# Attention output divided from a DRAM copy of the turned factors: twelve of sixteen divisions

## The chip, the cores and the metric

The kernel runs on one core of a Trainium2 chip. A core has five engines that run side by side, each with its own instruction order: TensorE (PE, with its weight loads shown as PEld), VectorE (DVE), ScalarE (ACT), GpSimd (POOL) and SyncE (SP), which here only issues transfers. They work on one on-chip memory (SBUF, 128 partitions) and on PSUM, the accumulators into which PE writes; DRAM is reached by DMA. The metric is the device time of one execution in microseconds (us). The kernel before takes 1926.52 us, the median of three runs (1925.0, 1926.52 and 1926.74).

## The reference

The model is a two-layer decoder trunk over 1024 tokens of width 1024: a short convolution with a SwiGLU mixer, then sliding-window attention with a SwiGLU mixer, all in float32. The change lies in the attention. There are 16 query heads of width 64, 4 key and value heads, a window of 128 tokens, a linear distance bias, and one learned logit per head (the sink) that takes part in the softmax and is then dropped:

```python
scores = jnp.einsum('bnqkgd,bnskd->bnkgqs', qb, kw).astype(jnp.float32) * scale
scores = scores + alibi[None, None]
scores = jnp.where(mask[None, :, None, None], scores, -jnp.inf)
logits = jnp.concatenate([scores, sink_col], axis=-1)
p = jax.nn.softmax(logits, axis=-1)[..., :-1]
out = jnp.einsum('bnkgqs,bnskd->bnqkgd', p.astype(vw.dtype), vw)
return out.reshape(bsz, s, N_Q_HEADS * HEAD_DIM) @ w_o
```

The kernel computes the exponents without dividing, multiplies them with the values, and divides the result afterwards by the sum of the exponents and the sink. This division is what the change rewrites.

## The kernel before, in words

Float32 products are made from pairs of a rounded high part and a low part (hi, lo), three matmuls for each product of two such pairs. The large matrix products also use a scheme with seven block products in place of eight.

**Layout.** Activations lie with features on the partitions and tokens along the free axis. Two heads make one tile i (0 to 7), two tiles make a pair p (0 to 3), and 1024 tokens make 8 blocks b of 128. The attention outputs of a pair lie in `O[p, h]` for each half h of the tokens (4 blocks).

**Steps.** The attention stage runs through 64 units (i, b), one for each step n, so a pair takes 16 steps. An order written out by hand, `ORDER = "SPTMEDkPHLVOPK"`, says what a step issues, and all engines keep the order in which they are issued (a manual schedule). S are the scores of unit n (PE, L2231 and L2232), M the row maxima (DVE, L2246), E the exponents of unit n-1 with their row sums (ACT, L2266), T the transposes of unit n-2 (PE, L2274) into one of the PSUM banks P1 and P3, in turn; the other of the two is called free in that step. H and L are the hi and lo parts of what T turned (ACT, L2281; DVE, L2287). V is the product with the values of unit n-3 (PE, L2300 and L2301) and O its copy into `O[p, h]` (ACT, L2318; DVE, L2319). Each P is a piece of other work for PE: the query product of a later pair (L1997), which from step 46 on gives way to the output product (L172, L176). D runs the list of this step's divisions, and k and K run work that was planned for this half or whole step: the normalisation of queries (L1803, L1808, L1813), the splitting of weight granules into hi (DVE, L1940) and lo (POOL, L1941), and of query tiles into hi (ACT, L2164) and lo (POOL, L2169).

**One division before.** A division takes a pair p, a half h of the tokens and a quarter k, at step n = 16p + 16 + 6h + 2k. At n-4 the sink goes into the sum (POOL, ACT, POOL; L2329 to L2331, only for k = 0). At n-2 DVE takes the reciprocal of the sums (L2336, 128x16, only for k = 0), and POOL spreads the factors over 512 columns in a buffer `s1` (L1803): query on the partitions, one column for each head and feature. At n PE turns that with four 128x128 transposes (L1808) into the free bank, and DVE multiplies `O` by what stands in the bank (L2347). The normalisation of the queries uses the same transposes, with a multiply by DVE (L1813).

**Transfers.** SP issues the operand loads of the query product (L2455, 512 KB from `q_ops` each) and the granules of the weights (L1934, 256 KB each). SP issues a transfer once its waits are over, and what stands behind waits with it. ACT issues none in this stage.

Of the kernel before, what the change touches and what calls it, by code (L numbers as in the profile page):

```python
# [47 lines left out]
SUB = P // 2  # L48
# [30 lines left out]
HALF = T // 2  # L79
# [9 lines left out]
def trunk_kernel(ctx: ExitStack, tc: tile.TileContext, xT, small, w_in, w_out, w_q, w_v, w_o, w_gu, w_dn, out):  # L89
    nc = tc.nc  # L90
    sb = ctx.enter_context(tc.tile_pool(name="sb", bufs=1))
    pm = ctx.enter_context(tc.tile_pool(name="pm", bufs=1, space=bass.MemoryType.PSUM))
    dve, act, pool, pe = nc.vector, nc.scalar, nc.gpsimd, nc.tensor
    uid = [0]

    def slot(tag, shape=(P, D), dtype=F32, bufs=1):
        uid[0] += 1
        return sb.tile(list(shape), dtype, tag=tag, name=f"{tag}_{uid[0]}", bufs=bufs)
# [107 lines left out]
    ident = cst[:, C_ID : C_ID + P]  # L206
# [1453 lines left out]
    def attention_layer():  # L1660
# [48 lines left out]
        def head_newton(y, t, m):  # L1709
            dve.scalar_tensor_tensor(t, t, -0.5, m, ALU.mult, ALU.mult)  # L1710
            dve.scalar_tensor_tensor(y, t, 1.5, y, ALU.add, ALU.mult)

        it = {}
        v = []
        summed = {}
# [183 lines left out]
        sums = {}  # L1899
# [421 lines left out]
        def divide_steps(p, h, k):  # L2321

            it = {}

            def sink():

                t = least[p, h]
                tiles = sinks[:, 2 * p : 2 * p + 2]
                pool.tensor_tensor(t, t, tiles.unsqueeze(1).to_broadcast([P, 8, 2]), ALU.subtract)  # L2329
                act.activation(t, t, AF.Exp)  # L2330
                pool.tensor_tensor(sums[p, h], sums[p, h], t, ALU.add)  # L2331

            def wide():
                d = sums[p, h]
                if k == 0:
                    dve.reciprocal(d, d)  # L2336
                it["wide"] = slot("s1", (P, HALF))
                spread(pool, it["wide"], d[:, 4 * k : 4 * k + 4, :])

            def rows():  # L2340
                it["ps"] = bank(pos["free"])
                turn_blocks(it["ps"], it["wide"])

            def scale():
                c = slice(k * 2 * P, (k + 1) * 2 * P)
                o = O[p, h][:, :, c].rearrange("p e (s q) -> p s e q", q=SUB)
                dve.tensor_tensor(o, o, it["ps"].rearrange("p (s e q) -> p s e q", s=4, q=SUB), ALU.mult)  # L2347

            return wide, rows, scale, sink


        due = {}
        divisions = {}
        for p in range(NK // 2):
            for h in (0, 1):
                for k in (0, 1):
                    *steps, sink = divide_steps(p, h, k)
                    divisions[p, h, k] = wide, rows, scale = steps
                    n = 16 * p + 16 + 6 * h + 2 * k
                    if k == 0:  # L2360
                        due.setdefault(n - 4, []).append(sink)
                    due.setdefault(n - 2, []).append(wide)
                    due.setdefault(n, []).extend([rows, scale])
        for n in due:
            due[n].sort(key=lambda f: f.__name__ == "wide")

# [2 lines left out]
        pos = {"n": -LAG, "step": 0, "free": "P1", "piece": 0, "values": None}  # L2369
        agenda = {}  # L2370

        def plan(d, f):

            agenda.setdefault(pos["step"] + d, []).append(f)
# [120 lines left out]
        with tc.manual_schedule(engines={E.PE, E.Activation, E.DVE, E.Pool, E.SP}):  # L2495
# [19 lines left out]
            todo = [late[0], late[1]]  # L2515
            free = ["XS4", "XS7"]
            first_w = {}
            for m in range(NK):
                acc = Acc()
                work = product(acc, w, o_split, len(early))  # L2520
                for k in range(len(early)):
                    if m + 1 < NK and k == 0:
                        w_next = Weights()
                        w_next.load(w_o[m + 1][:, 0 : len(early), :], 0, len(early))
                    if todo and pos["n"] >= 2 * NB * (todo[0] // 2 + 1) + 8:
                        split_o(todo.pop(0), free.pop(0), 0)
                    if m == NK - 1 and k == 0:
                        for t, tag in ((NK - 2, "XS0"), (NK - 1, "XS2")):
# [22 lines left out]
        for e in (0, 1):  # L2551
            wide, rows, scale = divisions[NK // 2 - 1, 1, e]
# [117 lines left out]
```

## Time and profile before

| | before |
|---|---|
| median of three runs | 1926.52 us |
| the profiled execution, own time | 1927.2 us |
| its span | 1925.2 us |
| PE busy | 1915.5 us (99%) |
| DVE busy | 1326.6 us (69%) |
| ACT busy | 894.0 us (46%) |
| POOL busy | 306.1 us (16%) |
| attention steps with divisions of pairs 0 to 2 | 1074 to 1204 us of the span |

The prediction reads the profile of this one execution. A group of instructions is named by its line, its engine and what it writes and reads. Behind a row, [0.43 <-DVE mx L2246] says that the engine sat idle for 0.43 us before this instruction, and that the wait ended with DVE's line 2246. In a timeline a row with x4 is four instructions in a run, with the time from the first start to the last end.

### The profile page before, as it was taken

How to read it: one execution, taken by the hardware profiler on the slowest of the kernel's cores; microseconds unless marked ns; L12 is line 12 of the kernel's file. 1: busy time of each engine (PE TensorE's matmuls, PEld its weight loads, DVE VectorE, ACT ScalarE, POOL GpSimd, SP SyncE). 2: the span in 40 equal slices, each digit the busy share in tenths (PEclk: the TensorE clock that was granted, in tenths of full speed). 3: DMA queues.
4: the chain of work that ended last, by engine and by line, in shares of the span. 5: the costliest groups of instructions: out<-in, count | busy, mean ns of one | idle time of the engine just before them, and what ended most of it. 6: DMA issues, size and time to landing. Idle time of an engine off the chain costs nothing.

```text
span 1925.2 us, 25420 instructions
## 1 busy us (share of the span) xinstructions
PE 1915.5 (99%) x9045; PEld 1599.9 (83%) x9045; DVE 1326.6 (69%) x2293; ACT 894.0 (46%) x1753; POOL 306.1 (16%) x391
## 2 busy tenths in 40 slices
PE   9999999999999999999999999999999999999999
PEld 7888888888888888888887888888888888888887
DVE  8997877975665666655866887788756665665543
ACT  5543464633333334444557787655333333344441
POOL 0011231011111100000015556310111111100000
PEclk9999999999999999999998999999999999999999
DMA  8897595387898638986364661242675575477562
GB/s 317 258 249 157 128 250 156 114 269 210 230 250 231 155 135 293 323 251 207 108 253 141 207 215 56 78 153 80 218 211 139 199 190 164 133 246 273 197 229 100
DMA packets 154910, 374.13 MB, mean 194 GB/s; under 512 B 15392, under 2 KB 26784, under 8 KB 154784
## 3 DMA queue, kind: packets, MB, share of 16 engines
q1 hardware_dynamic: 119392, 263.16, 39.8%
q0 software_dynamic: 35248, 109.33, 23.2%
q8 instruction: 71, 1.16, 0.2%
q14 instruction: 55, 0.45, 0.1%
q10 hardware_dynamic: 144, 0.03, 0.0%
HBM read 300.89 MB, written 149.42 MB: 234 GB/s over the span
## 4 chain that ended last, share of the span: by engine, by line
PE 95%; DVE 2%; ACT 2%; issue 1%; POOL 0%; DMA 0%; POOLq 0%; DVEq 0%; ACTq 0%
PE acc L1004 16%; PE acc L1007 16%; PE acc L1005 16%; PE P L1004 10%; PE P L1007 10%; PE P L1005 10%; PE acc L172 2%; PE acc L1997 2%; PE P L1997 2%; PE acc L176 1%; PE P L2274 1%; PE P L1678 1%; PE acc L1137 1%; PE acc L1139 1%; PE acc L1138 1%; PE P L1808 1%
## 5 line engine op out<-in xcount | busy, mean ns | idle before, releaser
L1004 PE MATMUL acc<-XS,G 128*128 128x512 f32 x926 | 360.4, 389 | 0.0
L1007 PE MATMUL acc<-XS,G 128*128 128x512 f32 x926 | 360.3, 389 | 0.0
L1005 PE MATMUL acc<-XS,G 128*128 128x512 f32 x926 | 360.2, 389 | 0.0
L1004 PE MATMUL P<-A,G 128*128 128x512 f32 x550 | 214.1, 389 | 0.0
L1007 PE MATMUL P<-A,G 128*128 128x512 f32 x550 | 214.0, 389 | 0.0
L1005 PE MATMUL P<-A,G 128*128 128x512 f32 x550 | 214.0, 389 | 0.0
L1007 PEld LDWEIGHTS acc<-XS,G 128*128 128x128 f32 x926 | 173.8, 188 | 36.2
L1005 PEld LDWEIGHTS acc<-XS,G 128*128 128x128 f32 x926 | 173.9, 188 | 36.0
L1004 PEld LDWEIGHTS acc<-XS,G 128*128 128x128 f32 x926 | 173.9, 188 | 35.9
L1004 PE MATMUL acc<-A,G 128*128 128x512 f32 x442 | 172.1, 389 | 0.0
L1007 PE MATMUL acc<-A,G 128*128 128x512 f32 x442 | 172.0, 389 | 0.0
L1005 PE MATMUL acc<-A,G 128*128 128x512 f32 x442 | 171.9, 389 | 0.0
L938 DVE TENSOR_TENSOR G<-WL,G 128x512 fp32r<-128x512 f32 x168 | 115.1, 685 | 73.5 <-ACT G L937 73.5
L938 DVE TENSOR_TENSOR G<-WR,G 128x512 fp32r<-128x512 f32 (+1 forms) x216 | 144.3, 668 | 29.3 <-ACT G L937 29.1
L937 ACT CAST G<-WR 128x512 fp32r<-128x512 f32 (+1 forms) x216 | 130.5, 605 | 63.2 <-PE acc L1007 30.7
L937 ACT CAST G<-WH 128x512 fp32r<-128x512 f32 (+1 forms) x174 | 104.7, 601 | 85.1 <-PE acc L1007 43.9
L1339 ACT ACTIVATE G<-G 128x512 f32<-128x512 f32 x88 | 55.8, 634 | 159.0 <-DVE G L1436 153.1
L938 DVE TENSOR_TENSOR G<-WH,G 128x512 fp32r<-128x512 f32 (+1 forms) x174 | 115.5, 664 | 20.4 <-ACT G L937 20.3
L1004 PEld LDWEIGHTS P<-A,G 128*128 128x128 f32 x550 | 103.3, 188 | 21.5 <-DVE G L548 0.2
L1007 PEld LDWEIGHTS P<-A,G 128*128 128x128 f32 x550 | 103.3, 188 | 21.5
L1005 PEld LDWEIGHTS P<-A,G 128*128 128x128 f32 x550 | 103.3, 188 | 21.3
L901 POOL DMA_DIRECT2D s<-s x68 | 60.0, 892 | 361.0 <-DMA s<-s 177.9
(414 smaller groups left out, 3806.1 us busy)
## 6 DMA issues: line engine op xcount, KB each, us to landing
G<-h SPq DMA_DIRECT2D x70, 512.0 KB, 4.8
s<-in_w_dn SPq DMA_DIRECT2D x32, 704.0 KB, 8.2
h<-X POOLq DMA_DIRECT2D x44, 512.0 KB, 5.2
s<-s POOLq DMA_DIRECT2D x32, 704.0 KB, 7.1
WR<-s SPq DMA_DIRECT2D x79, 256.0 KB, 3.9
WR<-in_w_gu SPq DMA_DIRECT2D x36, 512.0 KB, 5.2
WH<-in_w_gu SPq DMA_DIRECT2D x36, 512.0 KB, 4.6
XS<-q_ops SPq DMA_DIRECT2D x36, 512.0 KB, 5.3
```

The source lines that it names most:

```text
L172: pe.matmul(ps.half(h), wh, xs[:, j, c], start=first and j == 0, stop=False)
L176: pe.matmul(ps.half(h), wl, xs[:, 0, c], start=False, stop=last)
L901: nc.gpsimd.dma_start(dst[to], dst[of], accum_op=ALU.add)
L937: lambda: act.copy(out_hi, raw),
L938: lambda: lo_eng.tensor_tensor(out_lo, raw, plain(out_hi), ALU.subtract),
L1004: pe.matmul(ps, w[:, 0, c], x[:, 0, :], start=start and e == 0, stop=False, skip_group_check=True)
L1005: pe.matmul(ps, w[:, 0, c], x[:, 1, :], start=False, stop=False, skip_group_check=True)
L1007: pe.matmul(ps, w[:, 1, c], x[:, 0, :], start=False, stop=last, skip_group_check=True)
L1137: pe.matmul(ps, hi[:, kc], xs[:, 0, c], start=k == 0, stop=False, skip_group_check=True)
L1138: pe.matmul(ps, hi[:, kc], xs[:, 1, c], start=False, stop=False, skip_group_check=True)
L1339: state["silu"] = act.activation(x, x, AF.Silu)
L1997: pe.matmul(ps, g[:, w, c], x[:, b, :], start=begin and i == 0, stop=end and i == 2, skip_group_check=True)
```

## The change

The twelve divisions of pairs 0, 1 and 2 take another way; the four of the last pair stay. At n-3 DVE takes the reciprocal into a small buffer of its own (`hr_z`, 128x16). Half a step later PE turns it with one transpose into 16 rows of 128 (L1716 of the changed file), ACT copies it from PSUM into an `s1` buffer (L1718), and ACT's queue writes it to DRAM (L1719, 8 KB). One step after the reciprocal SP reads it back with two transfers (L1725), each of which gives one row of 512 factors to 64 partitions. The second quarter is read at n-1. POOL multiplies `O` by the buffer, at n+1 for the first quarter and at n+2 for the second. The spreading copies on POOL, the groups of four transposes and the multiplies on DVE are gone for these twelve. Two late splits of the output tiles wait for two more steps.

```diff
+        def rows_to_dram(columns, room, dst):
+            ps = bank(pos["free"])
+            pe.transpose(ps[0 : 2 * NB, 0:P], columns.rearrange("p h b -> p (h b)"), ident)
+            turned = room[0 : 2 * NB, 0:P]
+            act.copy(turned, ps[0 : 2 * NB, 0:P])
+            nc.scalar.dma_start(dst, turned)
+
+        def rows_from_dram(out, src, c=slice(0, D)):
+            for h in (0, 1):
+                row = src[h * NB : (h + 1) * NB].rearrange("b c -> (b c)")[c]
+                nc.sync.dma_start(out[h * HD : (h + 1) * HD, :], row.unsqueeze(0).to_broadcast([HD, row.shape[0]]))
...
             def scale():
                 c = slice(k * 2 * P, (k + 1) * 2 * P)
                 o = O[p, h][:, :, c].rearrange("p e (s q) -> p s e q", q=SUB)
-                dve.tensor_tensor(o, o, it["ps"].rearrange("p (s e q) -> p s e q", s=4, q=SUB), ALU.mult)
-
+                eng, by = (pool, it["wide"]) if divided_by_dma(p, h) else (dve, it["ps"])
+                eng.tensor_tensor(o, o, by.rearrange("p (s e q) -> p s e q", s=4, q=SUB), ALU.mult)
+
+            def inverse():
+                inv = slot("hr_z", (P, 2, NB), bufs=2)
+                dve.reciprocal(inv.rearrange("p i s -> p s i"), sums[p, h])
+                rows_dram[p, h] = tc.dram_tile((2 * NB, P), F32, name=f"rows_d{p}_{h}")
+                plan(0.5, lambda: rows_to_dram(inv, slot("s1", (P, HALF)), rows_dram[p, h]))
+                plan(1, fetch)
+
+            def fetch():
+                it["wide"] = slot("s1", (P, HALF))
+                rows_from_dram(it["wide"], rows_dram[p, h], slice(k * HALF, (k + 1) * HALF))
+
+            if divided_by_dma(p, h):
+                return inverse, fetch, scale, sink
             return wide, rows, scale, sink
...
+        def divided_by_dma(p, h):
+            return p < NK // 2 - 1
...
-                    due.setdefault(n - 2, []).append(wide)
-                    due.setdefault(n, []).extend([rows, scale])
+                    if not divided_by_dma(p, h):
+                        due.setdefault(n - 2, []).append(wide)
+                        due.setdefault(n, []).extend([rows, scale])
+                    elif k == 0:
+                        due.setdefault(n - 3, []).append(wide)
+                        due.setdefault(n + 1, []).append(scale)
+                    else:
+                        due.setdefault(n - 1, []).append(lambda f=rows: plan(0, f))
+                        due.setdefault(n + 2, []).append(scale)
...
-                    if todo and pos["n"] >= 2 * NB * (todo[0] // 2 + 1) + 8:
+                    if todo and pos["n"] >= 2 * NB * (todo[0] // 2 + 1) + 10:
```

In the instruction orders below, each row has the line, the operation, the buffer written and the buffers read, and the shape; lines of the changed file from 1712 on stand 14 or more higher than in the file before. `cst` is the identity for a transpose, `acc` and `P0` to `P3` are PSUM banks.

The first place is PE in step 20, which turns a normalisation of the queries (the group of four into P1, fed from G6). Before:

```order
L1997 MATMUL acc_1195_8416<-XS5_1115_7592,WL_1139_7846 128x512 x2
L2274 MATMUL P3_1307_9219<-cst_1_61,s0_1188_8369 128x128 x4
L1808 MATMUL P1_1310_9232<-cst_1_61,G6_1279_9037 128x128 x4
L1997 MATMUL acc_1195_8416<-XS5_1115_7592,WL_1139_7846 128x512
L1997 MATMUL acc_1195_8416<-XS7_1118_7619,WL_1139_7846 128x512
```

After the change:

```order
L2011 MATMUL acc_1195_8416<-XS5_1115_7592,WL_1139_7846 128x512 x2
L2288 MATMUL P3_1309_9220<-cst_1_61,s0_1188_8369 128x128 x4
L1822 MATMUL P1_1311_9231<-cst_1_61,G6_1282_9045 128x128 x4
L1716 MATMUL P1_1315_9242<-cst_1_61,hr_z_1302_9191 16x128
L2011 MATMUL acc_1195_8416<-XS5_1115_7592,WL_1139_7846 128x512
L2011 MATMUL acc_1195_8416<-XS7_1118_7619,WL_1139_7846 128x512
```

The single transpose of the factors stands right behind the group of four and writes the same bank P1. The same holds in step 36 for the next pair.

The second place is ACT in step 14. Before:

```order
L2266 ACTIVATE G2_1187_8368,den_1227_8630<-G2_1187_8368,mx_1223_8596 128x192 x2
L1973 COPY WR_1136_7843<-acc_1194_8415 128x512
L2281 CAST G0_1274_8988<-P3_1272_8971 128x512
L2318 COPY G8_1218_8569<-acc_1196_8417 64x2x2x64
```

After the change:

```order
L2280 ACTIVATE G2_1187_8368,den_1227_8630<-G2_1187_8368,mx_1223_8596 128x192 x2
L1718 COPY s1_1274_8984<-P1_1275_8985 16x128
L1719 DMA rows_d0_0_8942<-s1_1274_8984 16x128
L1987 COPY WR_1136_7843<-acc_1194_8415 128x512
L2295 CAST G0_1276_8993<-P3_1273_8974 128x512
L2332 COPY G8_1218_8569<-acc_1196_8417 64x2x2x64
```

The copy and the issue of the write stand ahead of a copy of the query product and of the cast of the turned exponents, which the values wait for. Steps 30 and 46 have the same for pairs 1 and 2.

The third place is SP around the first two reads. Before:

```order
L1934 DMA WR_1135_7842<-s4_104 128x512 x2
L2455 DMA XS6_1117_7606<-q_ops_105 128x2x512
L2455 DMA WH_1137_7844<-q_ops_105 128x1024
L2455 DMA XS0_1101_7500<-q_ops_105 128x2x512
```

After the change:

```order
L1948 DMA WR_1135_7842<-s4_104 128x512 x2
L2495 DMA XS6_1117_7606<-q_ops_105 128x2x512
L1725 DMA s1_1277_9008<-rows_d0_0_8942 64x512 x2
L2495 DMA WH_1137_7844<-q_ops_105 128x1024
L2495 DMA XS0_1101_7500<-q_ops_105 128x2x512
```

The two reads of the factors stand between two operand loads on the same queue.

More of the change, by code (lines that the diff above doesn't have):

```diff
@@ L2346, in scale @@
                 o = O[p, h][:, :, c].rearrange("p e (s q) -> p s e q", q=SUB)
-                dve.tensor_tensor(o, o, it["ps"].rearrange("p (s e q) -> p s e q", s=4, q=SUB), ALU.mult)
+                eng, by = (pool, it["wide"]) if divided_by_dma(p, h) else (dve, it["ps"])
[11 more added lines that the diff above has]
+                return inverse, fetch, scale, sink
             return wide, rows, scale, sink
+        rows_dram = {}
+        def divided_by_dma(p, h):
+            return p < NK // 2 - 1
         due = {}
```

## The prediction

> **What bounds the kernel now.** I read the page first: the busy shares, then the chain of work that ended last.
>
> ```profile
> span 1925.2 us, 25420 instructions
> PE 1915.5 (99%) x9045; PEld 1599.9 (83%) x9045; DVE 1326.6 (69%) x2293; ACT 894.0 (46%) x1753; POOL 306.1 (16%) x391
> ...
> PE 95%; DVE 2%; ACT 2%; issue 1%; POOL 0%; DMA 0%; POOLq 0%; DVEq 0%; ACTq 0%
> ```
>
> PE is busy for 99% of the span and carries 95% of the chain. Work taken off PE is therefore worth its own length, unless PE then waits. The average hides that the attention stage has little slack elsewhere, so I read busy times by stretch (length, then PE, PEld, DVE, ACT and POOL busy, PE's clock, DMA share, GB/s) and PE's waits from 1030 to 1260 us.
>
> ```profile
> 1071.00:1082.00 11.00, 10.56 (x73) 9.21 (x72) 10.19 (x29) 10.73 (x31) 8.07 (x7) 1.00 0.65 228
> 1090.00:1096.00 6.00, 6.00 (x45) 5.43 (x44) 5.84 (x18) 5.72 (x18) 2.64 (x5) 1.00 0.77 272
> 1193.00:1204.00 11.00, 10.95 (x73) 9.41 (x71) 9.40 (x28) 8.62 (x29) 5.27 (x6) 1.00 0.07 25
> ```
>
> ```profile
> PE acc L1997 <- POOL WL L1941: 1.7, 2, 1.4
> PE P L2231 <- DVE mx L2246: 1.6, 4, 0.4
> ```
>
> From 1071 to 1082 ACT is busy for 10.73 of 11.00 us and DVE for 10.19; from 1090 to 1096 PE, DVE and ACT are all nearly full. PE waits for DVE's maxima four times, 1.6 us together. So DVE and ACT stand right behind PE there, and a step gets shorter only where they let it.
>
> **What the change removes from PE.** Two steps of the output product, at the end of the divided stretch, give the price of a group of four transposes, because they differ by the group alone:
>
> ```profile
> 1197.85 0.25 PE L2231 MATMUL P<-A,G 128*128 128x192 f32 x1
> ...
> 1200.60 0.25 PE L2231 MATMUL P<-A,G 128*128 128x192 f32 x1
> ...
> 1201.94 0.60 PE L1808 MATMUL P<-cst,s 128*128 128x128 f32 x4
> ...
> 1203.79 0.25 PE L2231 MATMUL P<-A,G 128*128 128x192 f32 x1
> ```
>
> Both begin with the first scores (L2231). The step without a group lasts 1200.60 - 1197.85 = 2.75 us, the one with it 3.19. I take 0.43 (0.44 by these rounded starts): twelve groups give **-5.2 us**. Six single transposes come in at a quarter of a group, 0.11 each: **+0.65**. On PE alone the change is worth 4.5 us, or 0.24% of the time.
>
> **The bank of step 20 and of step 36.** In the changed order the single transpose of half 1 stands right behind a normalisation group and writes the same bank P1. It must wait until DVE has read that group out (L1813 in the same step); before, nothing wrote the bank then.
>
> ```profile
> 1093.87 0.60 PE L1808 MATMUL P<-cst,G 128*128 128x128 f32 x4
> 1094.22 0.71 PE L1997 MATMUL acc<-XS,WL 128*128 128x512 f32 x2
> ...
> 1142.88 0.71 PE L1997 MATMUL acc<-XS,WL 128*128 128x512 f32 x2
> ```
>
> ```profile
> 1094.81 0.25 DVE L2336 RECIPROCAL den<-den 128x16 f32<-128x16 f32 x1
> 1094.97 0.63 DVE L1813 TENSOR_TENSOR WH<-WH,P 128x512 f32<-128x512 f32 x1
> ...
> 1143.61 0.63 DVE L1813 TENSOR_TENSOR WH<-WH,P 128x512 f32<-128x512 f32 x1
> ```
>
> PE would issue the transpose at 1094.22; the read ends at 1095.60, or 1095.44 since the reciprocal ahead of it moves a step earlier. That is a wait of 1.22 us if PE came no earlier. But PE has by then saved two groups (n = 16 and 18) and paid one transpose, a lead of 0.75, and the lead is lost too if DVE does not come earlier with it. I assume it does not, since DVE is busy for 5.84 of the 6.00 us around it. That gives up to 1.97 a time; with the late ACT of the next term already eating 0.3 of the lead, I take 1.7 for each of the two steps, **+3.4 us**, with 2.4 (no lead lost) and 3.9 as ends. Behind the transpose on PE stand query-product matmuls and the values of that step, so the whole step moves. In step 36 the rows at 1142.88 and 1143.61 have the same distance: 1.36 us from PE's next matmul to the end of the read, against 1.38.
>
> **ACT's copy and write.** The trace has neither a 16x128 copy nor a DMA issue of ACT in this stage. The nearest copies and ACT's one DMA issue are (min, median and max in ns, then first and last start; the last line is the time from that issue to its landing):
>
> ```profile
> L1697 ACT ACTIVATE hr_y<-hr_m x10: 215/216/218, 994.2 to 1179.5; 128x16 f32<-128x16 f32 x10
> ...
> L2318 ACT COPY G<-P x16: 358/364/367, 1041.6 to 1135.5; 64x256 f32<-64x256 f32 x16
> ...
> L194 ACTq DMA_DIRECT2D cst<-in_small x1: 402/402/402, 0.7 to 0.7; - x1
> ...
> DMA to landing us min/median/max: 3.3/3.3/3.3
> ```
>
> 128 columns lie between 16 (0.22) and 256 (0.36), so 0.28 for the copy. The issue is bounded by 0 and 0.40 plus the wait for the copy's end; I take 0.3. Together 0.6 us in steps 14, 20, 30, 36, 46 and 52. In steps 20 and 36 it lies inside the bank wait. In step 14 it stands ahead of ACT's cast, and what waits for that is DVE, then PE (ACT's, DVE's and PE's timelines):
>
> ```profile
> 1075.56 0.58 ACT L2281 CAST G<-P 128x512 fp32r<-128x512 f32 x1
> ```
>
> ```profile
> 1076.17 0.69 DVE L2287 TENSOR_TENSOR G<-P,G 128x512 fp32r<-128x512 f32 x1
> ...
> 1077.35 1.09 DVE L1940 CAST WL<-WR 128x512 fp32r<-128x512 f32 x1
> ```
>
> ```profile
> 1079.52 0.27 PE L2231 MATMUL P<-A,G 128*128 128x64 f32 x1 [0.43 <-DVE mx L2246]
> ```
>
> The cast on ACT comes 0.6 later, DVE's subtraction behind it, DVE's cast and the maxima (L2246) behind that, and PE already waits for such maxima by 0.43 before step 16. I take +0.5 in step 14 and +0.5 in step 30 (the same place one pair later). The ends are +0.7 each (0.28 and 0.40 in full) and -0.43: POOL's spreading copy is gone there, so the cast of L1940, here 1.09 long, may be as short as 0.43 again (below), and PE's wait vanish. Step 46 is ACT-bound too:
>
> ```profile
> 1176.56 0.69 DVE L2287 TENSOR_TENSOR G<-P,G 128x512 fp32r<-128x512 f32 x1 [1.98 <-ACT G L2281]
> ...
> 1177.31 1.95 PE L1678 MATMUL P<-cst,XS 128*128 128x2 f32 x16 [0.16 <-DVE G L2287]
> ```
>
> PE waits at 1177.31 for DVE, which waits for ACT: +0.6, from 0 to 0.6. Together **+1.6 us** (-0.9 to +2.0). In step 52 ACT's copy has to wait for a free `s1` until POOL's multiply is through. ACT is busy there for 8.62 of 11.00 us (the last of the stretches above) and can catch up: **+0.2** (0 to 0.5).
>
> **DVE and POOL.** DVE loses twelve multiplies of 0.68 us (L2347). POOL swaps twelve copies (L1803) for multiplies whose nearest row is a subtraction of the same shape (L2429):
>
> ```profile
> L2347 DVE TENSOR_TENSOR G<-G,P x8: 681/682/689, 1081.6 to 1155.4; 128x512 f32<-128x512 f32 x8
> ```
>
> ```profile
> L1803 POOL COPY s<-den x16: 602/611/622, 1076.2 to 1248.9; 128x512 f32<-128x512 f32 x16
> ```
>
> ```profile
> L2429 POOL TENSOR_TENSOR XS<-G,XS x6: 1277/1294/1302, 1156.3 to 1169.1; 128x512 fp32r<-128x512 f32 x6
> ```
>
> ```profile
> L1940 DVE CAST WL<-WR x20: 411/428/1511, 1029.6 to 1160.4; 128x512 fp32r<-128x512 f32 x20
> ```
>
> ```profile
> 1184.75 0.63 PE L1808 MATMUL P<-cst,XS 128*128 128x128 f32 x4 [0.34 <-DVE A L2347]
> ```
>
> One multiply that PE waited for falls away, at 1184.75: **-0.34**. The other DVE time is gain only where DVE ended a wait of PE, and the waits for maxima other than those of steps 16 and 32 bound it at 1.6 - 0.86 = 0.7. Against it stand 12 x (1.29 - 0.61) = 8.2 us more of POOL, and the casts of L1940, 0.43 at the median and 1.51 at worst. The worst one ran while POOL was in a subtraction that ended at 1100.37:
>
> ```profile
> 1099.15 1.50 DVE L1940 CAST WL<-WR 128x512 fp32r<-128x512 f32 x1
> ```
>
> ```profile
> 1098.93 1.44 POOL L2169 TENSOR_TENSOR G<-WH,G 64x512 fp32r<-64x512 f32 x1 [0.40 <-ACT G L2164]
> ```
>
> After the stalls of steps 20 and 36 DVE also stands behind PE for some steps. For both I take **+0.6**, from -0.7 to 2.0. The Trainium skill ("SBUF — State Buffer", § Who interferes with whom) says that DVE and GpSimd share one port pair, locked by the one that issues first while the other fully blocks, and that copies and casts can take it. By that rule twelve multiplies, if each caught one cast, would cost DVE up to 12 x 0.7 = 8 us, an estimate that treats every cast as caught, and the sum would be +9 if all of it reached PE. The trace agrees on the mechanism (1.51 against 0.43), and shows it in two rows, 1077.35 (1.09) and this one.
>
> **The read-back on SP.** The three rows are an issue in SP's timeline, PE's first use of what it loads, and the median landing time of such loads (5.3 us). 24 reads join SP's queue ahead of operand loads, and the first one waits until ACT's write has landed.
>
> ```profile
> 1077.50 0.32 SPq L2455 DMA_DIRECT2D WH<-q_ops  x1
> ```
>
> ```profile
> 1086.61 0.62 PE L1997 MATMUL acc<-WH,WL 128*128 128x512 f32 x2
> ```
>
> ```profile
> XS<-q_ops SPq DMA_DIRECT2D x36, 512.0 KB, 5.3
> ```
>
> The load at 1077.50 stands behind the first reads. From it to its first use by PE (L1997 at 1086.61, which reads WH) there are 9.1 us, of which landing takes 5.3: 3.8 of slack, about what the write needs if it lands as ACT's one transfer did, 3.3 us after its issue. I cost the reads at **0**, hidden behind matmuls of operands loaded earlier; without that cover a write that lands late would push PE by what is over, 1 to 2 us in up to four places.
>
> **The sum.** -5.2 + 0.65 + 3.4 + 1.6 + 0.2 - 0.34 + 0.6 = **+0.9 us**. The profiled execution would go from a span of 1925.2 and an own time of 1927.2 to 1926.1 and 1928.1. The median before, 1926.52, lies 0.7 below that own time, so the changed kernel's median is **1927.4 us**. With all terms at their low ends (2.4, -0.9, 0, -0.7) the sum is -4.1, with all at their high ends (3.9, 2.0, 0.5, 2.0) +3.5.
>
> A measurement of this kernel can tell about 0.2%, 3.9 us, from no change: faster is below 1922.7, slower above 1930.4.
>
> **The rivals.** *The gain shows* (0.22). If DVE's read of the bank comes earlier with PE, or the late ACT falls into slack, only one bare bank wait of 1.2 and 0.5 of ACT may remain, and the maxima give 0.7: -5.2 + 0.65 - 0.34 + 1.2 + 0.5 - 0.7 = -3.9, **1922.6 us**. For it speaks that DVE loses 8 us of work; against it that PE, DVE and ACT are all full right where the bank wait falls.
>
> *PE's waits drop its clock* (0.13). The one long wait of the stage is followed by a stretch at half clock:
>
> ```profile
> 1035.60:1038.90 3.30, 1.88 (x15) 1.63 (x15) 1.97 (x6) 2.42 (x6) 2.11 (x2) 1.00 0.63 233
> 1039.00:1045.70 6.70, 6.70 (x26) 5.92 (x26) 3.54 (x14) 3.78 (x10) 4.29 (x4) 0.50 0.13 43
> ```
>
> PE was busy for 1.88 of 3.30 us, and the next 6.7 us ran at 0.50, which costs 3.35. New waits of 1.7 us are as long as the one there (1.4), so one or two such stretches of 3.4 us are possible: 0.9 + 3.4 = +4.3, **1930.8 us**. It decides once a wait leaves PE about 45% idle over 3.3 us. Against it: the steps around 20 and 36 have dense matmuls of 512 columns, while the quiet stretch also held 128x2 ones. The Trainium skill ("TensorE: Matmul & The Clock Gate", Part 1) says that the clock falls only after an idle window of about 3.4 us. By it no wait of 1.7 us would drop the clock, and this rival would be nought; the rows above, with PE busy for more than half, speak against so strict a reading.
>
> *The reads hold up SP* (0.15). If the write takes 4.7 us instead of 3.3, the load behind it lands 0.9 us past its use (3.8 of slack), and so in each of the six halves: 0.9 + 6 x 0.9 = +6.3, **1932.8 us**. It decides where PE's L1997 starts to wait for a DMA; before, it never does.
>
> That the change does what it says in instructions and still nothing in time, as what bounds the steps is ACT and the bank, is the forecast itself.
>
> **How the numbers follow.** The forecast of no difference holds 0.50; faster 0.22 and slower 0.28 are the others. The range reaches to 1922.0, past the value of the first rival, and to 1932.0, between the second and the third; the forecast's own is the sum's, 1922.4 to 1930.0.
>
> **What would show it.** Right: L1716 in steps 20 and 36 waits 1.5 to 2 us for DVE L1813, PE's wait at step 16 grows from 0.43 to about 0.9, and steps 18 and 34 are 0.43 shorter. Wrong: L1716 waits less than 1 us, PE rows at a clock of 0.50 between 1090 and 1150, or L1997 waiting for a DMA.

## The result, and the profile after

| | before | changed |
|---|---|---|
| median of six runs each | 1926.31 us | 1932.72 us |
| ratio, 95% interval | | 1.0036 (1.0024 to 1.0049) |
| span of the profiled execution | 1925.2 us | 1930.7 us |

The change makes the kernel 6.4 us slower. That is outside the range, and near the time of the third rival (1932.8), but by chance: its cause is not there, as shown below. From here on lines of the changed file stand 14 or more higher than in the file before: the scores are L2245, the maxima L2260, the granule's cast L1954 and its subtraction L1955, the normalisation's multiply L1827.

PE's work did become less, and its waits grew. The page after, then PE's waits from 1030 to 1260 us of the changed kernel (total, times, longest):

```profile
span 1930.7 us, 25359 instructions
PE 1911.3 (99%) x9003; PEld 1593.4 (83%) x9003; DVE 1320.6 (68%) x2281; ACT 893.8 (46%) x1759; POOL 313.9 (16%) x391
```

```profile
PE P L2245 <- DVE mx L2260: 8.4, 9, 1.6
PE P L1716 <- DVE WH L1827: 2.5, 2, 1.2
PE acc L2011 <- POOL WL L1955: 1.6, 2, 1.4
PE P L1678 <- DVE G L2301: 0.7, 1, 0.7
PE P L2314 <- DVE XS L2333: 0.4, 1, 0.4
```

Waits for the maxima went from 1.6 to 8.4 us, the bank's are new with 2.5, and none is for a DMA.

To see where they lie I cut the stretch from the first scores of step 14 to those of step 62 into four parts: its length, PE's idle time (the sum of all gaps before its matmuls), the time lost to half clock (half of what the windows show at 0.50), and the rest, PE's own work. Before: 151.87 = 1.69 idle + 0 at half clock + 150.18. After: 160.48 = 10.19 + 3.42 + 146.88 (rounded). So 3.3 us of work are saved, 8.5 us of idle time come in, and two stretches at half clock. Ahead of step 14 the execution after is 3.3 us shorter, and it has none of the stretches at half clock that the execution before has at 1018 and 1039 us; so the two spans differ by 5.5 us and not by 8.6.

Idle time at the main places, before and after (at steps 20, 36 and 47 inside the step, at the others in front of its first scores): step 16, 0.43 and 1.60; step 20, 0 and 1.23; step 23, 0.28 and 0.55; step 32, 0.42 and 1.57; step 36, 0 and 1.22; steps 39, 41 and 44, 0 and 0.61, 0.60, 0.87; step 47, 0.16 and 0.66; step 62, 0 and 0.87. Four of these places show the four mechanisms. First ACT, DVE, POOL and PE of the changed kernel ahead of step 16, from their timelines:

```profile
1071.31 0.44 ACT L2280 ACTIVATE G<-G,mx 128x192 f32<-128x192 f32 x1
...
1071.96 0.25 ACT L1718 COPY s<-P 16x128 f32<-16x128 f32 x1
1072.24 0.33 ACTq L1719 DMA_DIRECT2D rows_d<-s  x1
1072.62 0.59 ACT L1987 COPY WR<-acc 128x512 f32<-128x512 f32 x1 [0.41 <-ACT s L1718]
1073.10 0.59 ACT L2295 CAST G<-P 128x512 fp32r<-128x512 f32 x1
```

```profile
1073.73 0.69 DVE L2301 TENSOR_TENSOR G<-P,G 128x512 fp32r<-128x512 f32 x1 [1.07 <-ACT G L2295]
...
1074.91 1.46 DVE L1954 CAST WL<-WR 128x512 fp32r<-128x512 f32 x1
```

```profile
1074.81 1.28 POOL L2183 TENSOR_TENSOR G<-G,G 64x512 fp32r<-64x512 f32 x1 [1.59 <-ACT G L2178]
```

```profile
1077.43 0.27 PE L2245 MATMUL P<-A,G 128*128 128x64 f32 x1 [1.60 <-DVE mx L2260]
```

The same place before the change, ACT and POOL:

```profile
1074.65 0.44 ACT L2266 ACTIVATE G<-G,mx 128x192 f32<-128x192 f32 x1
...
1075.09 0.56 ACT L1973 COPY WR<-acc 128x512 f32<-128x512 f32 x1
```

```profile
1076.18 0.61 POOL L1803 COPY s<-den 128x512 f32<-128x512 f32 x1 [1.03 <-DVE den L2336]
1076.88 2.71 POOL L2169 TENSOR_TENSOR G<-G,G 64x512 fp32r<-64x512 f32 x2
```

Two things add up here. Before, ACT's copy of the query product began 0.44 us after the second exponent did (1074.65 and 1075.09); after, the same copy begins 1.31 us behind it (1071.31 and 1072.62). So 0.87 us of ACT are lost to one copy of 0.25 and one issue of 0.33, and 0.29 of waits around them. Most of the waits, 0.21, lies ahead of the copy, which starts only when PE's transpose has ended (1071.92). And DVE's cast takes 1.46 us, not 1.09: POOL starts a subtraction 0.10 us ahead of it, where before it had started one 0.47 us ahead, and in both cases the cast ends 0.28 or 0.29 us after that subtraction.

The second mechanism is the bank, on PE and DVE in step 20:

```profile
1091.29 0.60 PE L1822 MATMUL P<-cst,G 128*128 128x128 f32 x4
1093.12 0.28 PE L1716 MATMUL P<-cst,hr_z 128*16 128x128 f32 x1 [1.23 <-DVE WH L1827]
```

```profile
1092.38 0.68 DVE L1827 TENSOR_TENSOR WH<-WH,P 128x512 f32<-128x512 f32 x1
```

The step lasts 4.58 us, not 2.96. The third is POOL's hold on DVE, ahead of step 44:

```profile
1166.03 1.21 DVE L1706 TENSOR_TENSOR hr_y<-hr_y,cst 128x16 f32<-128x16 f32 x1
```

```profile
1164.67 1.29 POOL L2362 TENSOR_TENSOR G<-G,s 128x512 f32<-128x512 f32 x1
1165.92 1.29 POOL L2469 TENSOR_TENSOR XS<-G,XS 128x512 fp32r<-128x512 f32 x1
```

An operation on 16 columns, 0.18 us elsewhere, takes 1.21: it starts 0.11 us after POOL's subtraction and ends with it. The fourth is the clock. The windows of the changed kernel before and in a stretch at half clock (length, then PE, PEld, DVE, ACT, POOL busy, clock, DMA):

```profile
1124.95:1128.35 3.40, 1.82 (x12) 1.38 (x12) 3.31 (x8) 3.30 (x10) 2.70 (x3) 1.00 0.97 262
1128.35:1131.75 3.40, 3.40 (x13) 2.92 (x13) 1.63 (x6) 1.92 (x7) 1.14 (x1) 0.52 0.86 260
```

The wait of 1.57 us ahead of step 32 leaves PE busy for 1.82 of 3.40 us, and 3.4 us at half clock follow (they begin at 1128.5, a little inside the second window, so that its clock reads 0.52); 1.7 us are lost. The wait of 1.60 us ahead of step 16 is followed by none in this execution. The kernel before has such stretches too, at 1018 and 1039 us. They come and go between executions of one kernel: of 93 runs of the kernel before beside these experiments, 26 have a granted clock of 0.999 and a median span of 1922.95, 47 have 0.998 and 1923.9, 18 have 0.997 and 1925.15, and two have 1.000. The mean clock is 0.9981 before (3.6 us of a span) and 0.9973 over the six runs after (5.2 us). By these means about 1.6 of the 6.4 us are clock, and the rest, about 5, is the 8.5 of waits less the 3.3 of work. This is an estimate, since the clocks are rounded, and time at half clock can take the place of a wait: the six runs of the changed kernel have spans of 1930.5 and 1930.7 at 0.998 and of 1930.6, 1930.7, 1931.0 and 1932.4 at 0.997.

### The profile page after: what moved, and what is told of

It is laid out like the page before. It is cut to its first block, busy times and chain, and to the rows that moved or that the text cites. A ratio compares the mean times of both kernels' runs of the same rounds, so it can differ in the third digit from the quotient of the medians.

```text
span 1930.7 us, 25359 instructions
## 1 busy us (share of the span) xinstructions
PE 1911.3 (99%) x9003; PEld 1593.4 (83%) x9003; DVE 1320.6 (68%) x2281; ACT 893.8 (46%) x1759; POOL 313.9 (16%) x391
## 4 chain that ended last, share of the span: by engine, by line
PE 93%; DVE 4%; ACT 1%; issue 1%; POOL 1%; ACTq 0%; POOLq 0%; DVEq 0%
PE acc L1004 16%; PE acc L1007 16%; PE acc L1005 16%; PE P L1004 10%; PE P L1007 10%; PE P L1005 10%; PE acc L172 2%; PE P L2011 2%; PE acc L2011 2%; PE acc L176 1%; PE P L1678 1%; PE P L2288 1%; PE acc L1137 1%; PE acc L1139 1%; PE acc L1138 1%
```

## The experiments

Each is timed beside the kernel before, whose median was 1925.5 to 1926.3 us each time. The ratios are given as recorded and may differ a little from the quotient of two medians. Length, idle time and the time lost to half clock are those of step 14 to 62 in the profile of each run. Idle time and half clock must be read together, because a PE at half clock comes later to what it would have waited for. In six runs (second half later, before without division, sink on DVE, sink later, both moved, no multiply) PE runs at half clock just ahead of step 44 and shows no wait there, where the run with both edits waits for 1.04 us.

| run | median us | ratio to before (95%) | length | idle | half clock |
|---|---|---|---|---|---|
| changed kernel | 1932.72 | 1.0036 (1.0024 to 1.0049) | 160.48 | 10.19 | 3.42 |
| DVE multiplies | 1937.91 | 1.0066 (1.0051 to 1.0081) | 163.53 | 12.66 | 3.42 |
| second half a step later | 1931.82 | 1.0030 (1.0019 to 1.0041) | 157.83 | 6.83 | 5.13 |
| not on ACT | 1927.90 | 1.0013 (1.0003 to 1.0022) | 154.79 | 6.49 | 1.70 |
| before without the groups | 1927.44 | 1.0007 (0.9998 to 1.0016) | 153.74 | 3.58 | 3.41 |
| both edits | 1925.75 | 0.9997 (0.9987 to 1.0006) | 151.48 | 5.06 | 0 |
| only the issue moved | 1929.38 | 1.0013 (1.0004 to 1.0023) | 156.42 | 7.93 | 1.71 |
| before without division | 1923.57 | 0.9985 (0.9976 to 0.9994) | 150.22 | 3.18 | 1.70 |
| both, sink on DVE | 1925.39 | 0.9995 (0.9986 to 1.0004) | 151.99 | 4.19 | 1.71 |
| both, one multiply earlier | 1925.90 | 1.0001 (0.9992 to 1.0010) | 152.77 | 4.74 | 1.71 |
| both, sink later | 1925.09 | 0.9996 (0.9987 to 1.0005) | 151.07 | 3.37 | 1.71 |
| both, multiply and sink moved | 1924.39 | 0.9992 (0.9983 to 1.0001) | 150.78 | 3.17 | 1.71 |
| both, no multiply | 1925.18 | 0.9995 (0.9985 to 1.0004) | 151.74 | 3.99 | 1.71 |

**The multiply on DVE.**

```diff
-                eng, by = (pool, it["wide"]) if divided_by_dma(p, h) else (dve, it["ps"])
+                eng, by = (dve, it["wide"]) if divided_by_dma(p, h) else (dve, it["ps"])
```

> As the changed kernel, but DVE multiplies by the rows read back, in place of POOL. Theory A (POOL's multiplies of 1.29 us lock DVE's casts out and keep POOL late): PE's waits for the maxima at steps 39, 41 and 44 (0.61, 0.60, 0.87) go and the time falls by 2 to 2.5 us, to about 1930.5. Theory B (ACT's copy and write, and the bank, make the whole loss; DVE has no room for twelve multiplies of 0.69): no gain or up to 1 us slower, 1932.5 to 1933.5.

5.2 us slower than the changed kernel; neither theory foresaw the size, and the waits that theory A wanted gone are 0.62, 0.89 and 0.67 us. So DVE is no better place for the multiplies; what they cost on POOL this run does not tell. The multiply of DVE stands ahead of the bank's read, and PE now waits 2.2 us in step 20 and again in step 36. The group of these multiplies (min, median, max in ns) shows the rest:

```profile
L2362 DVE TENSOR_TENSOR G<-G,s x8: 690/1209/1726, 1084.4 to 1170.7; 128x512 f32<-128x512 f32 x8
L2362 DVE TENSOR_TENSOR A<-A,s x4: 686/688/1799, 1197.2 to 1225.9; 128x512 f32<-128x512 f32 x4
...
L2362 DVE TENSOR_TENSOR XS<-XS,P x4: 687/689/689, 1243.4 to 1262.5; 128x512 f32<-128x512 f32 x4
```

With the factors in PSUM (last row) a multiply takes 0.69 us without exception; with both inputs in SBUF it takes up to 1.8.

**The second half one step later.** No group of four then stands ahead of the transpose in its bank.

```diff
-                plan(0.5, lambda: rows_to_dram(inv, slot("s1", (P, HALF)), rows_dram[p, h]))
-                plan(1, fetch)
+                plan(0.5 + h, lambda: rows_to_dram(inv, slot("s1", (P, HALF)), rows_dram[p, h]))
+                plan(1 + h, fetch)
```

> As the changed kernel, but the transpose, the copy and the write of each second half, and its first read, come one step later, where no group of four stands ahead of the transpose in the same bank. Theory A (the bank wait of steps 20 and 36 costs 1.6 us each on top of everything else): the two waits of 1.23 us and what goes with them vanish, 3.0 to 3.3 us less, 1929.5. Theory B (DVE and ACT hold those steps anyway, so that the wait only moves to the next maxima): less than 1 us, 1932.

The two bank waits are gone and idle time falls by 3.36 us, as theory A says, but the waits for the maxima at steps 23 and 39 grow from 0.55 and 0.61 to 0.95 and 1.04 us, and this profile has three stretches at half clock between steps 14 and 62, one more than the changed kernel. The median falls by 0.9 only, which is theory B's number. The run-by-run clock shows why: five of the seven runs have 0.995 and spans of 1929.5 to 1930.3; one has 0.997 and 1928.1, one 0.999 and 1926.3. At 0.997 the changed kernel has 1930.6 to 1932.4, so at the same recorded clock this one run is 2.5 us or more shorter. Theory A holds for the waits, and the median does not show it.

**Copy and write off ACT.**

```diff
-            act.copy(turned, ps[0 : 2 * NB, 0:P])
-            nc.scalar.dma_start(dst, turned)
+            dve.tensor_copy(turned, ps[0 : 2 * NB, 0:P])
+            nc.sync.dma_start(dst, turned)
```

> As the changed kernel, but DVE copies the turned factors out of PSUM and SP's queue issues the write; ACT does neither. Theory A (ACT's copy and issue ahead of the cast of the exponents make the 1.6 us waits of steps 16 and 32, and these drop PE's clock): 1.2 us less at each, 0.5 at step 47, and the two stretches at half clock (1.5 and 1.3) gone: 4 to 5 us less, 1928. Theory B (the cast of the granule behind POOL makes these waits): the waits stay at 1.2 us or more, and the time within 1.5 us of 1932.7.

As theory A has it, 4.8 us less. The waits of steps 16 and 32 fall from 1.60 and 1.57 to 0.76 and 0.77, that of step 47 is gone, and so is the half-clock stretch behind step 32. What stays at step 16 is DVE's cast, 1.52 us long in this run.

**Only the issue off ACT.** The second line of that edit alone:

```diff
-            nc.scalar.dma_start(dst, turned)
+            nc.sync.dma_start(dst, turned)
```

> As the changed kernel, but only the issue of the write moves from ACT's queue to SP's; ACT still copies the factors out of PSUM. Theory A (the issue and the wait for the copy ahead of it are most of ACT's delay): the waits of steps 16 and 32 fall from 1.6 to about 1.1 and the time by 2 us, 1930.5. Theory B (the copy's wait for PE is the delay): they stay at 1.5, 1932.5.

The waits of steps 16 and 32 are 1.07 and 1.08 and the time falls by 3.3 us: of the 0.8 us of wait that went with copy and issue together, the issue is about 0.5, the copy the rest. The times alone do not tell this run from the one before it, as their ratios to the kernel before are equal (1.0013). The share in the time is larger than in these waits, since the stretch at half clock behind step 32 went with them.

**The kernel before without the groups of four.**

```diff
             def rows():
-                it["ps"] = bank(pos["free"])
-                turn_blocks(it["ps"], it["wide"])
+                it["ps"] = it["wide"]
+                if p == NK // 2 - 1:
+                    it["ps"] = bank(pos["free"])
+                    turn_blocks(it["ps"], it["wide"])
```

> The kernel before without the twelve groups of four transposes; DVE multiplies by the unturned buffer, so the attention output of pairs 0 to 2 is divided by wrong factors and the kernel leaves this part of the division out. Nothing is added. Theory A (PE sets the pace, a group is worth 0.43 us): 5.2 us less than before, 1921.2. Theory B (DVE and ACT stand right behind PE): only half or less of it shows, 1923.5 to 1925.

Taking 48 transposes off PE gains nothing here, 1.0007, which is above the numbers of both theories. PE's work falls by 3.4 us in the profile, idle time grows by 1.9, and two stretches at half clock (3.41) come in. The mean clock of its ten runs is 0.9967, 6.3 us of a span against 3.6 before. But this run does not only take away. DVE's multiply now has both inputs in SBUF, and seven of the twelve take 0.86 to 1.78 us where they took 0.68 to 0.69 with the factors in PSUM, 4.9 us more of DVE in all:

```profile
L2349 DVE TENSOR_TENSOR G<-G,s x8: 686/1324/1785, 1079.7 to 1156.3; 128x512 f32<-128x512 f32 x8
```

So it does not tell alone what the transposes were worth. The next run, which adds nothing, does that better.

**The kernel before without the twelve divisions**, as the bound on any other way (`wide`, `rows` and `scale` return at once for pairs 0 to 2):

```diff
+                if p < NK // 2 - 1:
+                    return
```

> The kernel before without the division of pairs 0 to 2: no reciprocal, no spreading copy, no transposes and no multiply for these twelve; their attention output stays undivided. It is a bound on what any other way to divide could gain. Theory A (PE's transposes were hidden behind DVE, which is why leaving them out alone gained nothing): without DVE's multiplies too the gain shows, 5 us less than before, 1921. Theory B (ACT and half-clock stretches hold these steps): 1923.5 to 1925.5.

Leaving the twelve divisions out (only the sink's three operations stay) gains 2.4 us by the medians, 0.15% by the ratio, whose interval reaches from 1.2 to 4.6 us. That is less than the 5.2 us reckoned for the transposes alone, and just inside theory B's numbers. It is what the removal gains with the rest of the schedule as it is; a rearranged schedule was not tried without the division. PE's work falls by 4.84 us (0.40 a group), but the waits of steps 16 and 32 double (0.81 and 0.80), and those of steps 23 and 39 go from 0.28 and 0 to 0.66 and 0.65. DVE and POOL of this run ahead of step 16:

```profile
1077.28 1.46 DVE L1940 CAST WL<-WR 128x512 fp32r<-128x512 f32 x1
```

```profile
1077.17 1.28 POOL L2169 TENSOR_TENSOR G<-G,G 64x512 fp32r<-64x512 f32 x1 [0.70 <-ACT G L2164]
```

In the kernel before POOL waited for the reciprocal, copied, and only then began the subtraction at 1076.88. Without the copy that subtraction is over before the cast, and the next one, which waits for ACT, begins just ahead of it (by 0.11 us). Less of it is over when the cast begins, and the cast takes 1.46 us where it took 1.09. So DVE's cast behind POOL, more than ACT, holds these steps.

**Both edits together** (the second half later, nothing on ACT):

> The changed kernel with both edits together: the second half's transpose one step later, and the copy on DVE with the write on SP's queue. Theory A (bank wait and ACT's delay are separate costs): PE's waits from step 14 to 62 fall from 10.2 us to about 3.5, and the time is 1924 to 1926, no different from before or up to 2 us faster. Theory B (POOL's longer work brings the waits back at other maxima): waits of 6 us or more, 1928.

Its edit is the two diffs named. 7.0 us less than the changed kernel, no different from before, so with these two causes the loss against the kernel before goes too. The work saved on PE (3.8 us) is still eaten by idle time, 5.06 us for 1.69. The time is as theory A has it. Idle time falls by 5.1, less than the 3.4 and 3.7 of the single edits added up, and not to the 3.5 of theory A, because waits of 0.56 and 0.86 at steps 23 and 39 and of 1.04 at 44 are there; this profile has no stretch at half clock.

**The sink of the last pair.** Step 62 waits 0.87 us in the changed kernel: POOL's late splits hold the sink's subtraction, ACT's exponent waits for it, and ACT's cast behind it. POOL before, then POOL and ACT after:

```profile
1214.55 1.29 POOL L2429 TENSOR_TENSOR XS<-A,XS 128x512 fp32r<-128x512 f32 x1 [0.21 <-ACT XS L2428]
...
1221.42 0.22 POOL L2329 TENSOR_TENSOR mx<-mx,cst 128x16 f32<-128x16 f32 x1 [3.14 <-ACT G L2266]
```

```profile
1224.22 2.55 POOL L2469 TENSOR_TENSOR XS<-A,XS 128x512 fp32r<-128x512 f32 x2
1226.73 0.22 POOL L2343 TENSOR_TENSOR mx<-mx,cst 128x16 f32<-128x16 f32 x1
```

```profile
1226.97 0.22 ACT L2344 ACTIVATE mx<-mx 128x16 f32<-128x16 f32 x1 [0.83 <-POOL mx L2343]
```

Two tries on top of both edits, DVE in POOL's place, and POOL one step later:

```diff
+                eng = dve if (p, h) == (NK // 2 - 1, 0) else pool
-                pool.tensor_tensor(t, t, tiles.unsqueeze(1).to_broadcast([P, 8, 2]), ALU.subtract)
+                eng.tensor_tensor(t, t, tiles.unsqueeze(1).to_broadcast([P, 8, 2]), ALU.subtract)
```

> As the run with both edits, and DVE in place of POOL subtracts the sink for the first half of the last pair, in step 60. Theory A (POOL, kept busy by the later splits, makes this subtraction late, and ACT's exponent, its cast and the maxima behind it make PE wait 0.87 us before step 62): this wait goes, 0.9 us less than that run. Theory B (the wait comes from DVE's own work there): no difference.

```diff
-                        due.setdefault(n - 4, []).append(sink)
+                        due.setdefault(n - (3 if (p, h) == (NK // 2 - 1, 0) else 4), []).append(sink)
```

> As the run with both edits, but only the sink of the last pair's first half comes one step later, behind POOL's late splits and behind ACT's cast. Theory A (ACT's exponent, waiting for POOL, holds the cast, and so PE before step 62): the wait of 0.87 us goes or falls below 0.2, 0.8 us less. Theory B (the wait is DVE's and stays whatever the sink does, as when DVE subtracted it): 0.7 us or more stays.

The first leaves 0.76 us and seemed to speak for DVE. Its DVE and POOL rows say otherwise:

```profile
1218.65 0.57 DVE L2344 TENSOR_TENSOR mx<-mx,cst 128x16 f32<-128x16 f32 x1
```

```profile
1216.64 2.56 POOL L2470 TENSOR_TENSOR XS<-A,XS 128x512 fp32r<-128x512 f32 x2
```

DVE's 16 columns end at 1219.22, POOL's splits at 1219.20: the engine changed, the wait for POOL did not. With the sink later the wait is gone in the profile (1.0 us off step 61). The median moves by 0.7, inside the interval.

**One multiply earlier.**

```diff
-                        due.setdefault(n + 2, []).append(scale)
+                        due.setdefault(n + (1 if (p, h) == (1, 1) else 2), []).append(scale)
```

> As the run with both edits, but one of POOL's twelve multiplies, that of pair 1, half 1, second quarter, comes one step earlier (41 in place of 42), into time in which POOL idles. Theory A (this multiply pushes a POOL subtraction onto a small DVE operation with two inputs from SBUF, L1706, which takes 1.21 us there in place of 0.18, and PE waits 1.04 us before step 44 for it): L1706 is back to 0.2 us, the wait goes, and the time falls by 0.9 to 1.0 us. Theory B (ACT's cast behind the multiply is what is late): L1706 stays long or the wait stays above 0.5 us.

A miss: L1706 still takes 1.22 us and the wait is 0.76, since POOL's next subtraction moved up into the multiply's place, to 1158.96, ahead of L1706 at 1159.07. So theory B's sign came, and that it was this multiply alone that pushed POOL onto L1706 is not shown.

**Both moves:**

> The run with both edits, with the earlier multiply and with the sink of the last pair's first half one step later (step 61, all three operations on their engines as before). If the two waits are separate costs: 1.9 us less than the run with both edits, 1923.9, which is 0.1% below the kernel before. If the clock's half-speed stretches decide instead: within 0.5 us of 1925.5.

Its edit is the last two, the sink's later step and the earlier multiply. 1924.39 us, 1.2 below the kernel before on the same chip (1925.61), with an interval that just reaches 1: unclear. That is 0.5 us above the first forecast and 1.1 below the second. In its profile L1706 takes no longer than 0.18 us, though the same earlier multiply alone did not bring that. It is the best version found that divides, and clearly faster than the change (1932.72). The spans of its eleven runs show what decides at this size: 1920.0, 1920.0 and 1920.5 at a clock of 1.000, 1923.8 to 1924.6 at 0.996.

**Both edits without multiplies:**

```diff
             def scale():
+                if divided_by_dma(p, h):
+                    return
```

> The run with both edits without POOL's twelve multiplies (the factors are written and read back, but the attention output of pairs 0 to 2 stays undivided). Theory A (what is left of the loss in the run with both edits is POOL's multiplies, which hold DVE's operations and POOL's own next ones): PE's waits from step 14 to 62 fall from 5.1 to about 3.2, the value without any division, and the time to 1923.5. Theory B (the waits left come from work that was there before, DVE's cast behind POOL's subtraction above all): they stay above 4.5, and the time within 0.7 us of 1925.75.

0.6 us less, as theory B has it, with idle time of 3.99, between the two. The waits at 16, 23, 32, 39 and 62 stay within 0.03 us of those in the run with both edits; what is missing is the 1.04 us of step 44. There L1706 is short in this run:

```profile
L1706 DVE TENSOR_TENSOR hr_y<-hr_y,cst x8: 174/174/175, 1018.2 to 1179.7; 128x16 f32<-128x16 f32 x8
```

So without POOL's multiplies its subtraction does not meet L1706, and they are a small part of what is left. How much of the missing wait is this and how much the half clock ahead of step 44 is not separated.

## Why the prediction was wrong

The forecast was no difference (+0.9 us), and the change costs 6.4. The step that failed most is the term for DVE and POOL: +0.6 us was taken, and 3.2 us of waits came. ACT's term was too small as well (+1.6, measured 2.8 with the cast behind POOL in it), and the clock had no term in the sum (about 1.6 us by the mean clocks). These three make up about the 5.3 us between 1927.4 and 1932.7; that the groups saved 1.2 us less than reckoned and that the bank's waits were 0.9 shorter nearly cancel.

- **"Twelve groups give -5.2 us", with +0.65 for the single transposes.** As PE work nearly right: 0.40 a group without the division (predicted 0.43), and 3.3 us net measured in the changed kernel against 4.5. Steps 18 and 34, which were to be shorter by 0.43, are shorter by 0.27 and 0.29. As time it was wrong: leaving the division out whole gains 2.4, and leaving out the groups alone, with DVE's multiplies longer for it, nothing. The sentence that a step gets shorter only where DVE and ACT let it stood at the start, and the sum then took the whole 5.2.
- **The bank, +3.4.** Right in size: 1.23 and 1.22 us of wait, and steps 20 and 36 longer by 1.62 each, 3.24 together. The place and the releaser (L1827) are as predicted; the waits themselves are below the 1.5 to 2 us named. Counted as the prediction counts, from when PE would issue the transpose (0.35 us after the group began, 1091.64) to its start at 1093.12, PE loses 1.48 us, which is 0.26 above the bare wait of 1.22; 0.5 was taken for the lost lead.
- **ACT's copy and write, +1.6.** The mechanism was right, the size not. Steps 16 and 32 wait 1.17 and 1.15 us more, where 0.5 each was taken and 0.7 was the high end. The copy (0.25) and the issue (0.33) are near the estimates of 0.28 and 0.3; what was left out are the waits around them, 0.29, so that ACT loses 0.87 us. With both off ACT 0.76 and 0.77 us of wait stay, so about 0.8 of the growth at each step is ACT's and the rest the cast's. The cast of L1940 was to become shorter when POOL's copy ahead of it goes; it became longer, 1.46 for 1.09. That was a misreading of the rows: the copy had ended at 1076.79, ahead of the cast, and what held the cast was the subtraction at 1076.88. Step 47 has 0.50 for the predicted 0.6.
- **DVE and POOL, +0.6 (to 2.0).** This term failed most: 0.61, 0.60 and 0.87 us at steps 39, 41 and 44, 0.87 at 62 and 0.27 at 23, 3.2 together. At 41 and 44 DVE's operations behind POOL's are stretched more than before (the cast 1.53 us for 0.89, L1706 1.21 for 0.18). At 23 and 39 the casts are stretched in both kernels (1.50 and 1.02 before, 1.06 and 1.11 after), and in the run not on ACT, where they are not, neither wait is there; why PE waits more for them than before is not separated, but the run without division, which adds no work, does so too (0.66 and 0.65). At step 62 it is POOL's splits, which now run just ahead of the sink. Their limit was raised by two steps (+ 10 for + 8), and that had no term at all. The prediction counted two stretched casts and called the one of 1.50 the worst; the kernel before has seven of twenty, the longest 1.51 at 1056.20. For this the Trainium skill's rule ("SBUF — State Buffer", § Who interferes with whom), that one of DVE and GpSimd blocks fully while the other holds the shared port pair, is borne out: the small operation with two inputs in SBUF ends with POOL's instruction (1219.22 and 1219.20), the cast 0.28 us after it (1076.37 and 1076.09), and the multiply with one input in PSUM is never stretched (0.681 to 0.689 in the kernel before, where 10 of 16 begin inside an instruction of POOL).
- **Step 52, +0.2.** Measured 0.13 in step 52 and 0.63 in step 53: ACT waits 1.26 us there for POOL's multiply, and PE 0.36 behind it.
- **The wait of 0.34 at step 48** went, as predicted.
- **The rival of the clock** was taken as one more case (0.13), with +3.4. It is part of every case: the kernel before loses 3.6 us to half clock on average, the changed one about 5.2. The place was right, as a stretch begins behind the wait of step 32, and so the sign named for being wrong is there, PE rows at 0.50 between 1090 and 1150. The condition, PE about 45% idle over 3.3 us, is not what decides: PE was idle for 0.15 of 3.41 us ahead of one stretch (last section), and for 1.47 of the 3.41 us from 1073.90, in step 16's wait, with no stretch behind them.
- **The rival of the reads on SP** came nearest in time, by chance, and is refuted: PE never waits for a DMA, and the write lands 1.4 us after its issue at the median, not 4.7. The reads land in 3.6 us.

What stays open is how much POOL's extra time costs in each step, as every edit moves the collisions, and what brings about a stretch at half clock in one run and not in the next.

## What to carry to other kernels

Where the bound engine waits for nothing but its neighbours are full, run the kernel once without the work to be saved: here that was worth 2.4 us where 5.2 were reckoned, before any cost of the change. Leave it out whole: without the transposes alone, DVE's multiplies read SBUF and grew by 4.9 us, and nothing of the gain was left. A small operation put into a gapless engine's order costs more than its length, since what it waits for stands in the queue with it. When moving work between VectorE and GpSimd, look at which operations of the two overlap, not at their sums: the same cast took 0.43 or 1.5 us.

## What was not expected of the hardware

Relieving POOL can make DVE slower. A cast of 0.43 us takes 1.46 to 1.53 when POOL begins a two-input operation 0.1 us ahead of it, and 1.09 when POOL had begun 0.47 us ahead. With the copy gone it was the next subtraction of POOL that met the cast, 0.36 us nearer to its start, and this cost DVE 0.37. What counts is how much of POOL's instruction is left: all seven stretched casts of the granule before, and all seven after, end 0.28 or 0.29 us behind it. In the run not on ACT two casts begin 0.07 and 0.16 us ahead of POOL's subtraction; they take 0.41 us, and the subtraction 1.49 and 1.40 in place of 1.28. In the run without the groups the multiply with two inputs in SBUF, 0.69 us alone, ends 0.55 behind it, and L1706, 0.17 alone, 0.03 behind it in the changed kernel. So in these traces all but about 0.14 us of DVE's operation comes after POOL's instruction has ended.

The half clock does not need idle time. It lasts 3.4 us (1018.45 to 1021.85 before; from 1128.5 to 1131.9 after) or twice that (the 6.7 us from 1039 in the prediction's row). In the run of the kernel before without the groups PE is busy for all but 0.15 of the 3.41 us ahead of such a stretch (windows as above), with sixteen 128x2 matmuls (L1678) among its work:

```profile
1176.89:1180.30 3.41, 3.26 (x27) 2.89 (x26) 2.00 (x6) 2.01 (x7) 2.85 (x4) 1.00 0.23 76
1180.30:1183.70 3.40, 3.40 (x13) 3.02 (x13) 1.95 (x8) 2.15 (x8) 0.00 (x0) 0.50 0.00 1
```

The Trainium skill ("TensorE: Matmul & The Clock Gate", Part 1) has a free-running window of 3413 ns, and the lengths of 3.4 us agree with such a window. That the clock falls only after an idle window of that length is not what these rows show; what in PE's work decides it was not tried.
